# A two-layer hybrid-attention trunk on one NeuronCore: the first loads come as single blocks in the order of their use, and the rotary step works on both query tiles at once

## The chip, the cores and the metric

The kernel runs on one core of a Trainium2 chip. The metric is device time in microseconds (us), the median of several executions. The core has a matrix engine (TensorE, PE in the rows), whose weight loads are listed apart (PEld), a vector engine (VectorE, DVE), an activation engine (ScalarE, ACT), a general engine (GpSimd, POOL) and a sync engine (SP) that here only issues transfers (DMA) from DRAM to on-chip memory. Every engine works through its own instructions strictly in the order of the program; engines wait for each other and for transfers by semaphores.

## The reference, cut to what matters

One sequence of 256 tokens with 1024 channels goes through two layers. `h @ w_in` is one large projection whose column groups feed three attention branches; the rotary step (`apply_partial_rope`) turns the first 16 of 64 channels of some heads.

```
def apply_partial_rope(x, cos, sin):
    half = ROPE_DIM // 2
    xr = x[..., :ROPE_DIM].astype(jnp.float32)
    x1, x2 = xr[..., :half], xr[..., half:]
    rot = jnp.concatenate([x1 * cos - x2 * sin, x2 * cos + x1 * sin], axis=-1)
    return jnp.concatenate([rot.astype(x.dtype), x[..., ROPE_DIM:]], axis=-1)
...
    h = rms_norm(x, norm_g)
    proj = h @ w_in
...
    return x + merged @ w_out
```

## The kernel before, in words

The 256 tokens are two query tiles of 128 (`NT` = 2, index `t`); the 1024 channels are eight blocks of 128 (`KD` = 8, index `k`). Every matrix product keeps nearly full float32 precision: both operands are split into a rounded high part and the rest, and three products are added up (`mm3`, lines 297 to 299: high by high, high by low, low by high). The activations' parts are `hT` and `lT`; the weights' parts are `wh` and `wl`. A weight tile is 1024 columns wide and holds two blocks of 512 columns, or two of 384 to 396 columns, or four of 256; it is loaded into `st` (`load`, line 251), ScalarE rounds it into `wh` (line 275), and VectorE subtracts to get `wl` (line 276). `split` does that, four tiles ahead of TensorE (`AHEAD`). For the first tile alone the split is done block by block (line 272).

The program begins with `begin()` of layer 0, then `warm()`, which clears a scratch page `z` on VectorE (line 389) and multiplies it by itself on TensorE (line 392), then `x_cols(k)`, which makes `hT` on ScalarE (line 403) and `lT` on VectorE (line 404) from a transposed copy of the input `xt`, scaled by the gains of the norm. The product of the first projection is called `a` (`ps_a`): 8 blocks by 2 tiles by 3 products of 512 columns, 48 matrix products in all. Then come `mv`, `b`, `mq` and others of 384 to 396 columns, and between them `w0` to `w3` (`mm_w1`, lines 757 and 758), which multiply by `Z`.

When `ps_a` is complete, `post_a` takes it out of the accumulators, which needs the norm's factor `rt` (lines 326 to 331). It then scales heads into `qn` (line 497 for many heads, line 508 for one key head that is written twice), turns them by `rope` on GpSimd (lines 447 to 452), and TensorE transposes them against the identity matrix (line 460). The key heads are called `ns` (from `a`) and `nw` (from `b`, in `post_b`). ScalarE then makes `kh` (line 489) and VectorE `kl` (line 490).

The order of TensorE's instructions is the order of the code, which places background work by a clock of its own. The instructions of the other engines are put in order by a scheduler when the program is built: it may move one instruction ahead of another that stands earlier in the code. So the order on an engine is not read from the code.

Of the kernel before, what the change touches and what calls it, by code (L numbers as in the profile page):

```python
# [9 lines left out]
F32 = mybir.dt.float32  # L10
F32R = mybir.dt.float32r
AF = mybir.ActivationFunctionType
ALU = mybir.AluOpType
# [4 lines left out]
KD = D // 128  # L18
# [58 lines left out]
def lay_out(inputs):  # L77

    big = ("x", "w_in", "b_gate", "cmp_w1", "w_up_moba", "w_up_nsa", "w_up_fox", "w_out")
    a = {n: np.ascontiguousarray(inputs[n]) for n in big}  # L80
    a["first"] = np.concatenate([np.eye(128, dtype=np.float32), inputs["norm_g"].reshape(L * KD, 128).T], 1)
# [12 lines left out]
@with_exitstack  # L94
def trunk(ctx, tc, x, w_in, b_gate, cmp_w1, w_up_moba, w_up_nsa, w_up_fox, w_out, first_d, x_t, small_d, row_d, out):
    nc = tc.nc
    V, A, G, T = nc.vector, nc.scalar, nc.gpsimd, nc.tensor

# [16 lines left out]
    po = ctx.enter_context(tc.tile_pool(name="po", bufs=1, space=PSUM))  # L115


    first = const.tile([128, 144], F32, name="first")
    nc.scalar.dma_start(first, first_d)
    ident, ngc = first[:, 0:128], first[:, 128:144]  # L120
    xs = [const.tile([128, D], F32, name=f"x{t}") for t in range(NT)]

    def load_x(t):
# [22 lines left out]
        return bass.AP(tensor=src.tensor, offset=src.offset + off, ap=[list(d) for d in dims])  # L146

    def small_loads():
        nc.sync.dma_start(tabs[:, K_COS:K_W2], small_d[:, K_COS:K_W2])
        nc.sync.dma_start(row, bcast(row_d, 0, (0, 128), (1, R_END)))  # L150

# [96 lines left out]
                out_ += [(w_, i) for i in range(w_["m"])]  # L248
        return out_

    def load(w_, eng):
        n = w_["n"]
        w_["st"] = wst.tile([128, 1024], F32, name="st")
        v = w_["st"][:, 0:w_["m"] * n].rearrange("p (k n) -> p k n", n=n)
        for r, a, b, src in w_["loads"]:
            eng.dma_start(v[r, a:b], src)

    def prefetch_loads(n):

        for w_ in tiles[:n]:  # L260
            load(w_, nc.scalar)

    def split(w_):
        if "st" not in w_:
            load(w_, nc.sync)
        n = w_["n"]
        c = w_["m"] * n
        sv = w_["st"][:, 0:c]
        wh = wsp.tile([128, 1024], F32R, name="wh")
        wl = wsp.tile([128, 1024], F32R, name="wl")  # L270
        w_["h"], w_["l"] = wh[:, 0:c], wl[:, 0:c]
        m = n if w_["at"] == 0 else c
        for i in range(0, c, m):
            h = w_["h"][:, i:i + m]
            A.activation(h, sv[:, i:i + m], AF.Copy)  # L275
            V.tensor_tensor(w_["l"][:, i:i + m], sv[:, i:i + m], h.bitcast(F32), op=ALU.subtract)  # L276

# [84 lines left out]
    def layer(l):  # L362
# [5 lines left out]
        def begin():  # L368
            if l == 0:
                x_loads()  # L370
                prefetch_loads(2)
            sh["pre"] = A.preload_act_table_set("natural_log_exp_and_others")
            after(sh["pre"], state["sigs"])
            sh["om"] = [pgs.tile([128, D], F32, name=f"om{i}", tag="page") for i in range(NT)]
            sh["ssq"] = sm.tile([128, NT], F32, name="ssq")
            sh["hT"] = new_T()
            sh["z"] = [pgs.tile([128, D], F32, name=f"z{t}", tag="page") for t in range(NT)]
# [8 lines left out]
        def warm():  # L386

            z = sh["z"][0][:, 0:256]
            V.memset(z, 0.0)
            ps = pat.tile([128, 512], F32, name="at")  # L390
            for _ in range(4):
                T.matmul(ps[:, 0:256], z[:, 0:128], z, start=True, stop=True)

        def x_loads():

            sh["xt"] = [pgs.tile([128, 4, S], F32, name="xt", tag="page") for _ in range(2)]
            for a, b in ((0, 2), (2, 4), (4, 8)):
                nc.sync.dma_start(sh["xt"][a // 4][:, a % 4:a % 4 + b - a, :], x_t[:, a:b, :])

        def x_cols(k):  # L400
            xt, h, lo = [a[:, k % 4, :] for a in (sh["xt"][k // 4], *sh["hT"][k // 4])]
            g = ngc[:, l * KD + k:l * KD + k + 1]
            A.activation(h, xt, AF.Copy, scale=g)
            V.scalar_tensor_tensor(lo, xt, g, h.bitcast(F32), op0=ALU.mult, op1=ALU.subtract)  # L404

        def start_r():
# [32 lines left out]
            V.tensor_tensor(rr, rr, sh["r"][:, :, None].to_broadcast([128, NT, nh]), op=ALU.mult)  # L439
            return rr  # L440

        def rope(q, key, t, nh):

            tab = sh["rtab"][key]
            a = wk.tile([128, 6, 16], F32, name="rp_a")[:, 0:nh]
            b = wk.tile([128, 6, 16], F32, name="rp_b")[:, 0:nh]
            G.tensor_tensor(a, q[:, :, 0:16], tab[:, t, 0, :][:, None, :].to_broadcast([128, nh, 16]), op=ALU.mult)
            G.tensor_tensor(b[:, :, 0:8], q[:, :, 8:16],
                            tab[:, t, 1, 0:8][:, None, :].to_broadcast([128, nh, 8]), op=ALU.mult)
            G.tensor_tensor(b[:, :, 8:16], q[:, :, 0:8],  # L450
                            tab[:, t, 1, 8:16][:, None, :].to_broadcast([128, nh, 8]), op=ALU.mult)
            G.tensor_tensor(q[:, :, 0:16], a, b, op=ALU.add)  # L452

        def cols_of(q, pairs, key):

# [34 lines left out]
            V.scalar_tensor_tensor(e, p3[:, 0, :], g, d.bitcast(F32), op0=ALU.mult, op1=ALU.subtract)  # L490

        def heads_scaled(ps, rr, col, nh, key):
            res = []
            for t in range(NT):
                q = wk.tile([128, 6, HD], F32, name="qn", bufs=4)[:, 0:nh]
                res.append(q)
                V.tensor_tensor(q, ps[t][:, col:col + nh * HD].rearrange("p (h d) -> p h d", d=HD),
                                rr[:, t, 0:nh][:, :, None].to_broadcast([128, nh, HD]), op=ALU.mult)
                if key in sh["rtab"]:
                    rope(q, key, t, nh)  # L500
            return res

        def shared_scaled(ps, col, rr, i, key):
            res = []
            for t in range(NT):
                q = wk.tile([128, 6, HD], F32, name="qn", bufs=4)[:, 0:2]
                res.append(q)
                V.tensor_scalar(q, ps[t][:, col:col + HD][:, None, :].to_broadcast([128, 2, HD]),
                                rr[:, t, i:i + 1], None, op0=ALU.mult)
                rope(q, key, t, 2)  # L510
            return res

        def new_ss():
            return sm.tile([128, NT, 8], F32, name="ss")
# [247 lines left out]
        def cmp_post():  # L762
# [20 lines left out]
            kc = sm.tile([16, 2, HD], F32, name="kc")[0:NCMP]  # L783
            vc = sm.tile([16, HD], F32, name="vc")[0:NCMP]
            ssc = sm.tile([16, 1], F32, name="ssc")[0:NCMP]
            rsc = sm.tile([16, 1], F32, name="rsc")[0:NCMP]
            jk = sm.tile([16, HD], F32, name="jk")[0:NCMP]
# [218 lines left out]
        def queue_loads():  # L1006
            for o in ORDER:
                name, b = o[:-1], int(o[-1])
                if name == "w":
                    parts[o] = load_w1(b)  # L1010
                else:
                    c0, n = PROJ[name]
                    m = 1 if l == 0 and o == "a0" else 2 if l == 0 and o == "a1" else 4
                    parts[o] = chunk([[(i, i + m, rows_of(w, 4 * b + i, 4 * b + i + m, c0, n))
                                       for i in range(0, 4, m)]], n)
            sh["gls"] = [load_gl(c) for c in range(6)]
            sh["ups"] = [load_up(n) for n in range(2)]
            sh["outs"] = load_out()
# [10 lines left out]
        def mm_first(starts):  # L1029
            ps = sh["ps_a"] = new_acc()  # L1030
            if l == 0:
                for k in range(KD):
                    dense(ps, sh["hT"], parts[f"a{k // 4}"][k % 4:k % 4 + 1], 512, ks=[k], ends=(k == 0, k == KD - 1))
                    if k + 4 < KD:
                        x_cols(k + 4)
                return
            for t in range(NT):
                finish(starts[t])
# [120 lines left out]
```

## Time and profile before

| what | us |
|---|---|
| median of three runs | 523.15 (523.08 to 523.24) |
| the profiled execution, its own time | 524.93 |
| its span, which all rows are counted in | 522.8 |
| TensorE busy, matrix products | 508.3 (97% of the span) |
| VectorE busy | 395.0 (76%) |
| ScalarE busy | 326.3 (62%) |
| GpSimd busy | 106.4 (20%) |

The busy share of TensorE comes from modelled ends of overlapping products, so it says that the engine is nearly always in use, not that it runs at its peak. The profiled execution took 2.1 us more than its span and 1.8 us more than the median.

### The profile page before, as it was taken

The numbers are of one execution on the slowest core, as the hardware profiler recorded it, in microseconds if no ns is written. First come the engines' busy times: TensorE is split into PE (matmuls) and PEld (weight loads), VectorE is DVE, ScalarE is ACT, GpSimd is POOL, SyncE is SP. The second block draws the span as 40 slices with busy tenths as digits, with TensorE's granted clock in tenths as the row PEclk, the third lists the DMA queues.
The fourth block names the chain that finished last, engine by engine and source line by source line (L and its number), as shares of the span: only waits on it lengthen the run. The fifth ranks groups of instructions, "written<-read, shape, count | busy, mean of one in ns | idle before, by whom it ended". The sixth has DMA issues, their size and how long they took to land.

```text
span 522.8 us, 8342 instructions
## 1 busy us (share of the span) xinstructions
PE 508.3 (97%) x2862; PEld 453.4 (87%) x2862; DVE 395.0 (76%) x804; ACT 326.3 (62%) x619; POOL 106.4 (20%) x166
## 2 busy tenths in 40 slices
PE   7999999999999999899999989999999999989997
PEld 4899899999888888788889979999988888878886
DVE  3898787789974558898487987768898754697953
ACT  4886686976584375644276966678756555655440
POOL 3754314000300004025102333030011000132300
PEclk8999999999999999999999989999999999999999
DMA  8998876445554433655447987546437542445502
GB/s 296 334 245 245 234 234 188 141 154 162 173 180 126 147 121 93 205 171 181 136 144 216 226 230 218 178 135 197 158 120 213 170 123 83 160 131 192 180 21 80
DMA packets 56602, 90.73 MB, mean 174 GB/s; under 512 B 3696, under 2 KB 30960, under 8 KB 56560
## 3 DMA queue, kind: packets, MB, share of 16 engines
q1 hardware_dynamic: 55840, 89.08, 56.4%
q10 hardware_dynamic: 720, 1.12, 0.6%
q8 instruction: 22, 0.36, 0.3%
q14 instruction: 20, 0.16, 0.1%
HBM read 89.14 MB, written 1.05 MB: 173 GB/s over the span
## 4 chain that ended last, share of the span: by engine, by line
PE 67%; issue 15%; DVE 7%; POOL 5%; ACT 4%; DMA 1%; ACTq 0%; DVEq 0%; POOLq 0%
PE acc L297 19%; PE acc L299 18%; PE acc L298 18%; DVE wl L276 3%; ACT wh L275 2%; PE at L568 2%; DMA st<-in_w_in_dram 1%; POOL qn L452 1%; DVE om L921 1%; PE at L550 1%; PE at L551 1%; PE at L348 1%; PE at L460 1%; PE o L758 1%; PE o L757 1%
## 5 line engine op out<-in xcount | busy, mean ns | idle before, releaser
L276 DVE TENSOR_TENSOR wl<-st,wh 128x1024 fp32r<-128x1024 f32 (+4 forms) x177 | 201.8, 1147 | 65.3 <-ACT wh L275 63.6
L275 ACT ACTIVATE wh<-st 128x1024 fp32r<-128x1024 f32 (+4 forms) x177 | 169.9, 966 | 98.4 <-PE acc L299 72.0
L297 PE MATMUL acc<-wh,hT 128*128 128x512 f32 (+3 forms) x576 | 223.8, 388 | 2.4 <-ACT wh L275 2.2
L299 PE MATMUL acc<-wh,lT 128*128 128x512 f32 (+3 forms) x576 | 210.4, 365 | 0.0
L298 PE MATMUL acc<-wl,hT 128*128 128x512 f32 (+3 forms) x576 | 209.7, 364 | 0.4 <-DVE wl L276 0.4
L299 PEld LDWEIGHTS acc<-wh,lT 128*128 128x128 f32 x576 | 108.6, 189 | 12.4 <-DVE lT L404 0.9
L297 PEld LDWEIGHTS acc<-wh,hT 128*128 128x128 f32 x576 | 109.4, 190 | 11.0 <-ACT wh L275 2.8
L298 PEld LDWEIGHTS acc<-wl,hT 128*128 128x128 f32 x576 | 109.4, 190 | 8.5 <-DVE wl L276 1.4
L563 ACT ACTIVATE p<-p,nm 128x128 f32<-128x128 f32 x80 | 35.5, 445 | 29.6 <-DVE nm L561 29.5
L920 POOL TENSOR_TENSOR z<-z,tmp 128x512 f32<-128x512 f32 x8 | 13.0, 1653 | 113.2 <-ACT tmp L917 113.2
L561 DVE CUSTOM_DVE_ANT_0 p<-at,tabs 128x128 f32<-128x128 f32 x80 | 24.1, 352 | 9.9 <-PE at L555 9.8
L956 POOL TENSOR_TENSOR mg<-mg,tmp 128x512 f32<-128x512 f32 x8 | 15.8, 1998 | 55.0 <-DVE tmp L955 55.0
L297 PE MATMUL acc<-wh,qkT 128*128 128x512 f32 x64 | 25.2, 394 | 0.0
L299 PE MATMUL acc<-wh,qkT 128*128 128x512 f32 x64 | 24.9, 390 | 0.0
L298 PE MATMUL acc<-wl,qkT 128*128 128x512 f32 x64 | 24.9, 389 | 0.0
L568 PE MATMUL at<-first,p 128*128 128x128 f32 x120 | 19.8, 274 | 0.3 <-ACT qkT L483 0.2
L660 POOL TENSOR_TENSOR om<-om,tmp 128x256 f32<-128x256 f32 x8 | 7.7, 985 | 58.1 <-DVE rs_a L330 50.3
L906 DVE SCALAR_TENSOR_TENSOR gl<-acc,rt,tmp 128x512 f32<-128x512 f32 x24 | 17.0, 743 | 1.1 <-PE o L580 1.1
L568 PEld LDWEIGHTS at<-first,p 128*128 128x128 f32 x120 | 15.0, 146 | 2.5 <-ACT qkT L483 0.6
L758 PE MATMUL o<-wl,Z 128*63 128x256 f32 x64 | 16.3, 289 | 0.9 <-DVE wl L276 0.9
L757 PE MATMUL o<-wh,Z 128*63 128x256 f32 x64 | 16.6, 295 | 0.0
L572 DVE COPY pt<-at 128x384 f32<-128x384 f32 x20 | 11.0, 551 | 7.0 <-PE at L568 6.8
(232 smaller groups left out, 710.0 us busy)
## 6 DMA issues: line engine op xcount, KB each, us to landing
st<-in_w_in_dram SPq DMA_DIRECT2D x54, 512.0 KB, 3.4
st<-in_w_in_dram SPq DMA_DIRECT2D x56, 384.0 KB, 3.9
st<-in_cmp_w_dram SPq DMA_DIRECT2D x32, 256.0 KB, 4.2
st<-in_w_out_dram SPq DMA_DIRECT2D x16, 512.0 KB, 3.8
st<-in_w_in_dram SPq DMA_DIRECT2D x8, 396.0 KB, 6.9
st<-in_w_in_dram SPq DMA_DIRECT2D x8, 390.0 KB, 3.3
tmp<-in_b_gate_dram SPq DMA_DIRECT2D x12, 256.0 KB, 4.4
st<-in_w_up_moba_dram SPq DMA_DIRECT2D x4, 512.0 KB, 3.7
```

Source lines behind the costliest of these rows:

```text
L275: A.activation(h, sv[:, i:i + m], AF.Copy)
L276: V.tensor_tensor(w_["l"][:, i:i + m], sv[:, i:i + m], h.bitcast(F32), op=ALU.subtract)
L297: T.matmul(ps, sh, wh, start=first, stop=False)
L298: T.matmul(ps, sh, wl, start=False, stop=False)
L299: T.matmul(ps, sl, wh, start=False, stop=last)
L561: V.tensor_tensor_reduce(out=u, in0=sp, in1=tabs[:, K_MASK + 256 - nk:K_MASK + 256], scale=-SCALE, scalar=BIG, op0=ALU.add, op1=ALU.min, a ...
L563: exps.append(A.activation(u, u, AF.Exp, bias=nm, scale=-1.0, accum_out=rsum[:, t, hb:hb + 1]))
L568: T.transpose(pts[:, s * 128:(s + 1) * 128], p[:, s * 128:(s + 1) * 128], ident)
L757: T.matmul(U, st, h, start=i == 0, stop=False)
L758: T.matmul(U, st, lo, start=False, stop=i == CL - 1)
L906: V.scalar_tensor_tensor(sh["gl"][t][b][:, n * 512:(n + 1) * 512], ps[t], sh["r"][:, t:t + 1], bg, op0=ALU.mult, op1=ALU.add)
L956: (G if b == 1 else V).tensor_tensor(m, m, tmp, op=ALU.add)
```

## The change

Three edits. The identity matrix and the norm's gains, one transfer before, become two, and the identity comes later. The first loads are issued as single blocks in the order in which the first projection uses them, from two queues, and the first four weight tiles (eight blocks) are split block by block; block 0 of `hT` is made on VectorE, and `warm()` has five products in place of four. The rotary step handles both query tiles in one set of four operations in place of two sets. Some small buffers get one copy in place of two.

```
-    first = const.tile([128, 144], F32, name="first")
-    nc.scalar.dma_start(first, first_d)
-    ident, ngc = first[:, 0:128], first[:, 128:144]
+    ngc = const.tile([128, L * KD], F32, name="ngc")
+    nc.scalar.dma_start(ngc, gains_d)
+    ident = const.tile([128, 128], F32, name="ident")
...
     def small_loads():
+        nc.sync.dma_start(ident, eye_d)
...
-    def load(w_, eng):
+    def load(w_, queues):
...
-        for r, a, b, src in w_["loads"]:
-            eng.dma_start(v[r, a:b], src)
-
-    def prefetch_loads(n):
-
-        for w_ in tiles[:n]:
-            load(w_, nc.scalar)
+        for i, (r, a, b, src) in enumerate(w_["loads"]):
+            queues[i % len(queues)].dma_start(v[r, a:b], src)
...
-        m = n if w_["at"] == 0 else c
+        m = n if w_["at"] < 4 else c
...
-                prefetch_loads(2)
...
-            for _ in range(4):
+            for _ in range(5):
                 T.matmul(ps[:, 0:256], z[:, 0:128], z, start=True, stop=True)
...
-            for a, b in ((0, 2), (2, 4), (4, 8)):
+
+            def xk(a, b):
                 nc.sync.dma_start(sh["xt"][a // 4][:, a % 4:a % 4 + b - a, :], x_t[:, a:b, :])
+            xk(0, 1)
+            load(tiles[0], (nc.scalar, nc.sync))
+            xk(1, 2)
+            xk(2, 3)
+            load(tiles[1], (nc.scalar, nc.sync))
+            xk(3, 4)
+            load(tiles[2], (nc.sync,))
+            xk(4, 8)
+            load(tiles[3], (nc.sync,))
...
-            A.activation(h, xt, AF.Copy, scale=g)
+            if k == 0:
+                V.tensor_scalar(h, xt, g, None, op0=ALU.mult)
+            else:
+                A.activation(h, xt, AF.Copy, scale=g)
...
-        def rope(q, key, t, nh):
+        def rope(q, key, nh):
...
-            G.tensor_tensor(a, q[:, :, 0:16], tab[:, t, 0, :][:, None, :].to_broadcast([128, nh, 16]), op=ALU.mult)
...
+            G.tensor_tensor(a, q[:, :, :, 0:16], tb(0, 0, 16), op=ALU.mult)
+            G.tensor_tensor(b[:, :, :, 0:8], q[:, :, :, 8:16], tb(1, 0, 8), op=ALU.mult)
+            G.tensor_tensor(b[:, :, :, 8:16], q[:, :, :, 0:8], tb(1, 8, 16), op=ALU.mult)
+            G.tensor_tensor(q[:, :, :, 0:16], a, b, op=ALU.add)
...
         def shared_scaled(ps, col, rr, i, key):
...
+            q = wk.tile([128, NT, 2, HD], F32, name="kn", bufs=1)
+            for t in range(NT):
+                V.tensor_scalar(q[:, t], ps[t][:, col:col + HD][:, None, :].to_broadcast([128, 2, HD]),
                                 rr[:, t, i:i + 1], None, op0=ALU.mult)
-                rope(q, key, t, 2)
-            return res
+            rope(q, key, 2)
+            return [q[:, t] for t in range(NT)]
...
-                    m = 1 if l == 0 and o == "a0" else 2 if l == 0 and o == "a1" else 4
+                    m = 1 if l == 0 and name == "a" else 4
...
-                    if k + 4 < KD:
-                        x_cols(k + 4)
...
-    for k in range(4):
+    for k in range(KD):
         layers[0]["x_cols"](k)
-        prefetch(k + 1)
+        prefetch(k // 2 + 1)
```

The order of instructions on the engines moves at three places that matter below. First, VectorE at the very start, before the change:

```order
L162 MEMSET ones_96 128x1
L389 MEMSET z_122 128x256
L404 SCALAR_TENSOR_TENSOR lT<-xt,first,hT 128x256
L276 TENSOR_TENSOR wl<-st,wh 128x512 x2
L404 SCALAR_TENSOR_TENSOR lT<-xt,first,hT 128x256
L276 TENSOR_TENSOR wl<-st,wh 128x1024
```

And VectorE at the same place with the change:

```order
L164 MEMSET ones_97 128x1
L273 TENSOR_TENSOR wl<-st,wh 128x512 x2
L385 MEMSET z_131 128x256
L410 TENSOR_SCALAR hT<-xt,ngc 128x256
L273 TENSOR_TENSOR wl<-st,wh 128x512
L413 SCALAR_TENSOR_TENSOR lT<-xt,ngc,hT 128x256 x3
L273 TENSOR_TENSOR wl<-st,wh 128x512
```

The clearing of the scratch page `z` stood second and now stands behind the low parts of weight blocks 0 and 1. TensorE's order begins with the products of `z`, five now, and then the first projection, as before.

Second, GpSimd in layer 1, where the key heads `nw` are turned, before the change:

```order
L447 TENSOR_TENSOR rp_a<-qn,rtab_nw 128x32
L448 TENSOR_TENSOR rp_b<-qn,rtab_nw 128x2x8
L450 TENSOR_TENSOR rp_b<-qn,rtab_nw 128x2x8
L452 TENSOR_TENSOR qn<-rp_a,rp_b 128x2x16
L447 TENSOR_TENSOR rp_a<-qn,rtab_nw 128x32
L448 TENSOR_TENSOR rp_b<-qn,rtab_nw 128x2x8
L450 TENSOR_TENSOR rp_b<-qn,rtab_nw 128x2x8
L452 TENSOR_TENSOR qn<-rp_a,rp_b 128x2x16
```

And with the change, with the next operation of GpSimd behind it:

```order
L459 TENSOR_TENSOR rp_a<-kn,rtab_nw 128x2x32
L460 TENSOR_TENSOR rp_b<-kn,rtab_nw 128x2x2x8
L461 TENSOR_TENSOR rp_b<-kn,rtab_nw 128x2x2x8
L462 TENSOR_TENSOR kn<-rp_a,rp_b 128x4x16
L459 TENSOR_TENSOR rp_a<-qn,rtab_mq 128x192
```

Four operations of double size stand in the place of eight; the first tile is ready only when both are.

Third, ScalarE in layer 0, behind the product `w1`, where it makes `kh` from the transposed heads `nw`, before the change (`sq` is the square of the projection `mq`):

```order
L275 ACTIVATE wh<-st 128x1024
L489 ACTIVATE kh_292<-at,tabs 128x128
L432 ACTIVATE sq<-acc,rt 128x384
L275 ACTIVATE wh<-st 128x1024
L275 ACTIVATE wh<-st 128x768
```

And with the change:

```order
L272 ACTIVATE wh<-st 128x1024
L499 ACTIVATE kh_305<-at,tabs 128x128
L272 ACTIVATE wh<-st 128x1024
L499 ACTIVATE kh_305<-at,tabs 128x128
L272 ACTIVATE wh<-st 128x768
```

The square `sq` no longer stands ahead of the next weight tile's high part.

## Rows read from the trace of the kernel before

**Rows 1.** The page, busy time of each engine (share of the span, instructions).

```profile
PE 508.3 (97%) x2862; PEld 453.4 (87%) x2862; DVE 395.0 (76%) x804; ACT 326.3 (62%) x619; POOL 106.4 (20%) x166
```

**Rows 2.** Whom TensorE waited for: total us, times, longest us.

```profile
PE at L460 <- POOL qn L452: 2.7, 4, 1.3
PE acc L297 <- ACT wh L275: 2.2, 1, 2.2
PE o L758 <- DVE wl L276: 0.9, 1, 0.9
```

**Rows 3.** Timeline of the start: start us, us, engine, line, out<-in; [idle before, releaser].

```profile
0.89 0.27 DVE L389 MEMSET z<- 128x256 f32 x1
...
1.22 3.64 PE L392 MATMUL at<-z 128*128 128x256 f32 x8 [1.22 <-DVE z L389]
...
6.40 0.63 ACT L275 ACTIVATE wh<-st 128x512 fp32r<-128x512 f32 x1 [0.67 <-DMA st<-in_w_in_dram]
...
7.08 0.50 PE L297 MATMUL acc<-wh,hT 128*128 128x512 f32 x1 [2.22 <-ACT wh L275]
...
18.50 0.39 PE L297 MATMUL acc<-wh,hT 128*128 128x512 f32 x1
...
21.22 0.33 PE L297 MATMUL acc<-wh,hT 128*128 128x384 f32 x1
```

**Rows 4.** Windows of the start: busy us of each engine, PEclk, DMA share, GB/s.

```profile
3.00:4.00 1.00, 1.00 (x4) 0.73 (x3) 0.00 (x0) 0.72 (x1) 0.96 (x2) 1.00 0.82 219
7.00:8.00 1.00, 0.70 (x2) 0.38 (x3) 0.69 (x1) 0.03 (x1) 0.00 (x0) 1.00 1.06 408
...
10.00:11.00 1.00, 1.00 (x4) 0.81 (x3) 0.12 (x1) 0.75 (x1) 0.00 (x0) 0.50 1.06 394
...
12.00:13.00 1.00, 0.79 (x3) 0.19 (x1) 1.00 (x3) 1.00 (x3) 0.17 (x1) 1.00 1.00 353
```

**Rows 5.** Transfers of the first 22 us: count, KB each, median us to landing.

```profile
xt<-in_x_t_dram SPq DMA_DIRECT2D x2, 256.0 KB, 4.6
...
first<-in_first_dram ACTq DMA_DIRECT2D x1, 72.0 KB, 4.5
```

**Rows 6.** Groups of the first 22 us by shape: busy us, mean ns | idle before.

```profile
L404 DVE SCALAR_TENSOR_TENSOR lT<-xt,first,hT 128x256 fp32r<-128x256 f32 x8 | 3.6, 476 | 4.6 <-ACT hT L403 4.6
...
L276 DVE TENSOR_TENSOR wl<-st,wh 128x512 fp32r<-128x512 f32 x2 | 1.4, 692 | 2.1 <-ACT wh L275 2.1
...
L275 ACT ACTIVATE wh<-st 128x512 fp32r<-128x512 f32 x2 | 1.3, 630 | 2.0 <-DMA st<-in_w_in_dram 2.0
```

**Rows 7.** Timeline of layer 0 behind the first projection.

```profile
22.54 0.37 ACT L428 ACTIVATE kv<-acc,rt 128x128 f32<-128x128 f32 x1 [0.27 <-DVE rt L331]
...
36.18 0.44 PE L460 MATMUL at<-first,qn 128*128 128x128 f32 x2 [0.34 <-POOL qn L452]
...
55.31 0.33 PE L758 MATMUL o<-wl,Z 128*63 128x256 f32 x1 [0.93 <-DVE wl L276]
```

**Rows 8.** Timeline of layer 1 where the heads `nw` are turned.

```profile
302.72 0.61 DVE L508 TENSOR_SCALAR qn<-acc,rr 128x128 f32<-128x128 f32 x2
303.15 0.25 POOL L447 TENSOR_TENSOR rp_a<-qn,rtab_nw 128x32 f32<-128x32 f32 x1 [10.83 <-DVE qn L508]
303.25 4.22 DVE L276 TENSOR_TENSOR wl<-st,wh 128x768 fp32r<-128x768 f32 x4
303.36 0.94 POOL L448 TENSOR_TENSOR rp_b<-qn,rtab_nw 128x16 f32<-128x16 f32 x1
...
304.27 1.19 POOL L450 TENSOR_TENSOR rp_b<-qn,rtab_nw 128x16 f32<-128x16 f32 x1
...
305.54 1.11 POOL L452 TENSOR_TENSOR qn<-rp_a,rp_b 128x32 f32<-128x32 f32 x1
...
306.70 0.33 PE L460 MATMUL at<-first,qn 128*128 128x128 f32 x1 [1.28 <-POOL qn L452]
...
308.32 0.46 PE L460 MATMUL at<-first,qn 128*128 128x128 f32 x1 [0.77 <-POOL qn L452]
```

**Rows 9.** Window of layer 1 right behind that place; columns as in rows 4.

```profile
309.00:312.00 3.00, 3.00 (x16) 2.90 (x15) 1.69 (x3) 2.22 (x4) 0.00 (x0) 0.54 1.09 225
```

More of the change, by code (lines that the diff above doesn't have):

```diff
@@ L80, in lay_out @@
     a = {n: np.ascontiguousarray(inputs[n]) for n in big}
-    a["first"] = np.concatenate([np.eye(128, dtype=np.float32), inputs["norm_g"].reshape(L * KD, 128).T], 1)
+    a["gains"] = inputs["norm_g"].reshape(L * KD, 128).T
+    a["eye"] = np.eye(128, dtype=np.float32)
     a["x_t"] = inputs["x"][0].T.reshape(KD, 128, S).transpose(1, 0, 2)
@@ L94, in trunk @@
 @with_exitstack
-def trunk(ctx, tc, x, w_in, b_gate, cmp_w1, w_up_moba, w_up_nsa, w_up_fox, w_out, first_d, x_t, small_d, row_d, out):
+def trunk(ctx, tc, x, w_in, b_gate, cmp_w1, w_up_moba, w_up_nsa, w_up_fox, w_out, gains_d, eye_d, x_t, small_d, row_d, out):
     nc = tc.nc
@@ L254, in load @@
         v = w_["st"][:, 0:w_["m"] * n].rearrange("p (k n) -> p k n", n=n)
-        for r, a, b, src in w_["loads"]:
-            eng.dma_start(v[r, a:b], src)
-    def prefetch_loads(n):
-        for w_ in tiles[:n]:
-            load(w_, nc.scalar)
+        for i, (r, a, b, src) in enumerate(w_["loads"]):
+            queues[i % len(queues)].dma_start(v[r, a:b], src)
     def split(w_):
         if "st" not in w_:
-            load(w_, nc.sync)
+            load(w_, (nc.sync,))
         n = w_["n"]
@@ L440, in head_factors, with tb @@
             return rr
-        def rope(q, key, t, nh):
+        def rope(q, key, nh):
             tab = sh["rtab"][key]
-            a = wk.tile([128, 6, 16], F32, name="rp_a")[:, 0:nh]
-            b = wk.tile([128, 6, 16], F32, name="rp_b")[:, 0:nh]
-            G.tensor_tensor(a, q[:, :, 0:16], tab[:, t, 0, :][:, None, :].to_broadcast([128, nh, 16]), op=ALU.mult)
[L448 to L452, printed above, removed]
+            def tb(i, c0, c1):
+                return tab[:, :, i, c0:c1][:, :, None, :].to_broadcast([128, NT, nh, c1 - c0])
+            a = wk.tile([128, NT, 6, 16], F32, name="rp_a", bufs=1)[:, :, 0:nh]
+            b = wk.tile([128, NT, 6, 16], F32, name="rp_b", bufs=1)[:, :, 0:nh]
+            G.tensor_tensor(a, q[:, :, :, 0:16], tb(0, 0, 16), op=ALU.mult)
+            G.tensor_tensor(b[:, :, :, 0:8], q[:, :, :, 8:16], tb(1, 0, 8), op=ALU.mult)
+            G.tensor_tensor(b[:, :, :, 8:16], q[:, :, :, 0:8], tb(1, 8, 16), op=ALU.mult)
+            G.tensor_tensor(q[:, :, :, 0:16], a, b, op=ALU.add)
         def cols_of(q, pairs, key):
@@ L492, in heads_scaled @@
         def heads_scaled(ps, rr, col, nh, key):
-            res = []
+            q = wk.tile([128, NT, 6, HD], F32, name="qn")[:, :, 0:nh]
             for t in range(NT):
-                q = wk.tile([128, 6, HD], F32, name="qn", bufs=4)[:, 0:nh]
-                res.append(q)
-                V.tensor_tensor(q, ps[t][:, col:col + nh * HD].rearrange("p (h d) -> p h d", d=HD),
+                V.tensor_tensor(q[:, t], ps[t][:, col:col + nh * HD].rearrange("p (h d) -> p h d", d=HD),
                                 rr[:, t, 0:nh][:, :, None].to_broadcast([128, nh, HD]), op=ALU.mult)
-                if key in sh["rtab"]:
-                    rope(q, key, t, nh)
-            return res
+            if key in sh["rtab"]:
+                rope(q, key, nh)
+            return [q[:, t] for t in range(NT)]
         def shared_scaled(ps, col, rr, i, key):
-            res = []
+            q = wk.tile([128, NT, 2, HD], F32, name="kn", bufs=1)
             for t in range(NT):
-                q = wk.tile([128, 6, HD], F32, name="qn", bufs=4)[:, 0:2]
-                res.append(q)
-                V.tensor_scalar(q, ps[t][:, col:col + HD][:, None, :].to_broadcast([128, 2, HD]),
+                V.tensor_scalar(q[:, t], ps[t][:, col:col + HD][:, None, :].to_broadcast([128, 2, HD]),
                                 rr[:, t, i:i + 1], None, op0=ALU.mult)
-                rope(q, key, t, 2)
-            return res
+            rope(q, key, 2)
+            return [q[:, t] for t in range(NT)]
         def new_ss():
@@ L782, in cmp_post @@
                              w2s[:, l, kv, c, :], start=c == 0, stop=c == 1)
-            kc = sm.tile([16, 2, HD], F32, name="kc")[0:NCMP]
-            vc = sm.tile([16, HD], F32, name="vc")[0:NCMP]
+            kc = sm.tile([16, 2, HD], F32, name="kc", bufs=1)[0:NCMP]
+            vc = sm.tile([16, HD], F32, name="vc", bufs=1)[0:NCMP]
             ssc = sm.tile([16, 1], F32, name="ssc")[0:NCMP]
             rsc = sm.tile([16, 1], F32, name="rsc")[0:NCMP]
-            jk = sm.tile([16, HD], F32, name="jk")[0:NCMP]
+            jk = sm.tile([16, HD], F32, name="jk", bufs=1)[0:NCMP]
             A.activation(vc, ps[0:NCMP, HD:2 * HD], AF.Copy)
```

## The prediction

> **What bounds the kernel now.** I read the busy shares first: TensorE is in use 97% of the span [rows 1]. In such a kernel only time in which TensorE stands still, or runs at its lower clock, can be won or lost. So I read next whom TensorE waited for [rows 2], then the timeline of the two places that the change touches, the start [rows 3 to 6] and the rotary step [rows 7, 8].
>
> At the start the reader should see three things. The scratch products begin at 1.22, right behind the clearing of `z` at 0.89, and are over long before the first weight block has landed: they cost nothing. The first real product starts at 7.08, released by the high part of weight block 0, which ScalarE began at 6.40 after waiting for the transfer. And the first projection ends at 21.22, where the 384-column products begin [rows 3]. At full clock its 48 products need 48 x 0.227 = 10.9 us (12 of them from 18.50 to 21.22 take 2.72), so 14.1 - 10.9 = 3.2 us of its 14.1 us are lower clock and waits; the granted clock was 0.50 at 10 to 11 us and 1.00 again at 12 to 13 [rows 4], that is 1.2 and 2.4 GHz.
>
> The rotary step makes TensorE wait 2.7 us in all [rows 2]: 1.28 + 0.77 for the two `nw` tiles of layer 1 [rows 8], 0.34 at 36.18 in layer 0 [rows 7], and the remaining 0.3 for `nw` in layer 0.
>
> **The start, step by step.** The order of VectorE decides it. `z` is now cleared behind the low parts of blocks 0 and 1, so the scratch products, which stand first on TensorE, wait for two weight blocks to land and be split, and all the real work waits behind them.
>
> When do blocks 0 and 1 land? Before, block 0 had landed by 6.4 [rows 3], with 72 KB, two input pieces of 256 KB and itself on the way, 840 KB. Now 8 KB of gains, 128 KB of input and two weight blocks of 256 KB must come, 648 KB. The 192 KB less are 0.5 us at 408 GB/s [rows 4]: 5.9. Bounds: 5.0, where the first input piece landed before (issue at 0.74 plus about 4.3; the median of two is 4.6 [rows 5]), and 6.4, if the number of pieces counts and not their bytes. I take 5.9, since the rate was steady once transfers flowed.
>
> Then two high parts at 0.63, one low part at 0.69 [rows 6], the clearing at 0.27 [rows 3] and some 0.1 of hand-overs: 5.9 + 1.26 + 0.69 + 0.27 + 0.1 = 8.2 us for the first scratch product, in place of 1.2. Four of them took 3.64 us [rows 3], 0.91 each, so five take 4.55, to 12.8. I let the clock rise as long after the engine's start as before (from 7.08 to between 11 and 12, say 4.2 us): it rises at 12.4, the last 0.4 runs at double speed, and the real products begin at 12.6. They find all parts ready. From 8.2 VectorE has one high part (some 0.4 us), six low weight parts and eight low input parts to make, 0.4 + 6 x 0.69 + 8 x 0.48 = 8.4 us [rows 6], about 1.05 us for each of the eight blocks, where TensorE takes 1.36 for each. Without that cover each late part would cost up to the 2.2 us of block 0 in [rows 2]; I count none. So the projection ends at 12.6 + 10.9 = 23.5 in place of 21.2: **+2.3 us**. With landing at 5.0 and the clock 0.7 us earlier it is +1.0; with landing at 6.4 and a clock that rises some 3 us later (seven products at 0.2 us more each) it is +4.0.
>
> This delay is passed on in full, since what TensorE waits for later hangs on its own earlier products. It wins a little back. Before, the first projection was done 1.3 us before `rt` let its accumulators be emptied (21.22 against 22.54 [rows 7]); now `rt` has 2.3 us more, so heads come earlier against TensorE's stream and the wait of 0.34 at 36.18 goes: **-0.3** (bounds 0 and -0.34).
>
> **The wait at 55.31** (0.93 for a low weight part [rows 7]) is fed by ScalarE, where the square of `mq` stood ahead of that weight tile's high part. It is moved behind it, but the `kh` on which both wait stays. I take **-0.4**, about half; bounds 0 and -0.93.
>
> **The rotary step in layer 1.** Eight GpSimd operations become four. An undisturbed one of 32 elements takes 0.25 us [rows 8], so one set would take some 1.2 us. But the next three took 0.94, 1.19 and 1.11: VectorE ran four low weight parts from 303.25 (4.22 us, 1.055 each), and GpSimd finished one operation behind each [rows 8]. VectorE's order there is unchanged. The merged set can start only behind the second `qn`, which ends at 303.33, no longer ahead of the first low part. Its four operations then end behind the four low parts, the last at about 303.25 + 4.22 + 0.2 = 307.7, in place of 306.7 for the first tile. TensorE, which before stood until 306.70 and then until 308.32, with three products between, stands once, until 307.7, does the same three products (0.5 us), and goes on at 308.2: **0**, bounds +0.9 and, if GpSimd slips through, -2.05 and the clock with it. The granted clock was 0.54 at 309 to 312 behind these two waits [rows 9]; that lost 3 x 0.46 = 1.4 us. A single stall of 2.2 us is as long as the two, so I keep that loss. `nw` in layer 0 has the same trade: 0, bounds -0.3 and +0.4. For the other heads GpSimd was done before TensorE asked; a merged set has the same work ahead of the same product.
>
> The new small buffers, and the identity that lands later, are needed first by the transposes behind `mv0`: nothing, hidden by the first projection's 48 products.
>
> **The sum:** +2.3 - 0.3 - 0.4 + 0 = +1.6 us on the profiled execution, whose own time is 524.93 for a span of 522.8; as a difference it goes on the median: 523.15 + 1.6 = **524.8 us**. A difference under about 0.2% (1.05 us) can't be told from no change.
>
> **Rivals.**
>
> *The merged rotary step pays (faster).* If GpSimd's four operations in layer 1 run undisturbed, they end near 303.4 + 1.4 = 304.8, before TensorE asks at 305.42 (306.70 - 1.28 [rows 8]). Then 2.05 us of waiting and the 1.4 us of clock are won: 524.8 - 3.5 = 521.3 us. For it speaks the 0.25 us of an undisturbed operation, against it the three stretched ones. It decides at whether VectorE's low weight parts run between 303.4 and 305.4.
>
> *The start costs little (no change).* Blocks 0 and 1 land at 5.0 and the clock rises early: +1.0 in place of +2.3, so 523.5 us, no change that can be measured. For it speaks that far fewer bytes stand ahead; against it the slow first microseconds, 219 GB/s at 3 to 4 us [rows 4], which smaller pieces don't shorten by themselves.
>
> *Small pieces load slower (slower still).* If the first 648 KB come at 219 GB/s in place of 408, that is 3.0 in place of 1.6 us, and everything behind moves: 524.8 + 1.4 = 526.2 us. Against it speaks that pieces of 256 KB already moved at 408 GB/s with others in flight [rows 4].
>
> The Trainium skill (DMA: Bandwidth & Descriptors, Bandwidth) speaks for this rival: it wants at least 1 MiB in a transfer and lists 138 GB/s at 64 KB and 341 at 1 MB. By an estimate of 200 GB/s from that page the first blocks would land some 1.6 us later and the time be 526.4 us; the trace does not agree, with 408 GB/s at 7 to 8 us [rows 4].
>
> **How the numbers follow.** The forecast has 0.60, the paying rotary step 0.15, the cheap start 0.15, slow loading 0.10. Slower by over 0.2%: 0.60 + 0.10 = 0.70; within: 0.15; faster: 0.15. The range takes in the cheap start, with a little of the rotary step's gain, and the slow loading: 522.2 to 526.7; it leaves out most of the rotary rival and the far end of the slow start, under 0.2 together.
>
> **What would show it.** Right: scratch products that begin near 8 us, behind two low weight parts; a first projection without waits at full clock that ends near 23.5; no wait for the rotary step at its first place in layer 0; one stall near 2 us for `nw` in layer 1, with GpSimd's operations stretched to about 1 us. Wrong: scratch products that are over before the first block has landed, a first projection that ends before 21 us, or a merged rotary set of under 2 us in layer 1.

## The result and the profile after

The changed kernel took 527.34 us (median of four runs, 526.31 to 527.46), the kernel before 523.19 (four runs); ratio 1.0069 [1.0052, 1.0085]. It is slower, by 4.1 us at the medians; 1.6 were forecast. Timed again later (run f1 below) it took 526.88 us (median of ten runs) beside 523.61 for 27 runs of the kernel before, ratio 1.0046 [1.0029, 1.0064]. Why the distance differs between these two is half of what follows. The profiled execution after took 526.31 us for a span of 524.5, the fastest of its four; the one before had taken 524.93, more than any of the four. So the two traces lie only 1.4 us apart (1.7 in span).

The page of the changed kernel, busy time of each engine, to be held against [rows 1]:

```profile
PE 505.7 (96%) x2864; PEld 453.3 (86%) x2864; DVE 396.9 (76%) x808; ACT 326.4 (62%) x621; POOL 96.7 (18%) x126
```

GpSimd has 40 instructions and 9.7 us less, the merged rotary step; it is not what bounds the kernel. Whom TensorE waited for in the changed kernel (as [rows 2]):

```profile
PE at L388 <- DVE z L385: 7.6, 1, 7.6
...
PE at L470 <- POOL kn L462: 2.6, 2, 2.4
PE at L470 <- POOL qn L462: 0.6, 1, 0.6
PE at L470 <- ACT nqT L695: 0.6, 1, 0.6
PE o L764 <- DVE wl L273: 0.5, 1, 0.5
```

The 7.6 us ahead of the scratch products are no loss by themselves, since no block had landed for most of them. The rest tells the story: `nw` in layer 1 (now in a tile `kn`) is one stall of 2.4 in place of 1.28 and 0.77, and two waits of 0.6 are new. The timeline of the start (as [rows 3]):

```profile
5.30 1.67 ACT L272 ACTIVATE wh<-st 128x512 fp32r<-128x512 f32 x3 [1.88 <-DMA st<-in_w_in_dram]
5.96 1.29 DVE L273 TENSOR_TENSOR wl<-st,wh 128x512 fp32r<-128x512 f32 x2 [5.10 <-ACT wh L272]
...
7.26 0.27 DVE L385 MEMSET z<- 128x256 f32 x1
...
7.59 4.53 PE L388 MATMUL at<-z 128*128 128x256 f32 x10 [7.59 <-DVE z L385]
...
11.66 0.69 PE L294 MATMUL acc<-wh,hT 128*128 128x512 f32 x1
...
22.54 0.37 ACT L437 ACTIVATE kv<-acc,rt 128x128 f32<-128x128 f32 x1 [1.34 <-DVE rt L328]
...
22.87 0.33 PE L294 MATMUL acc<-wh,hT 128*128 128x384 f32 x1
```

As forecast, `z` is cleared behind two low parts, the scratch products come behind the first blocks, and the first projection then runs without a wait. The first block is there at 5.30 (forecast 5.9), and the projection ends at 22.87 (forecast 23.5, before 21.22 [rows 3]), 1.65 us later. `rt` lets the accumulators be emptied at 22.54, where it did before [rows 7]; that the two agree to the hundredth is chance, since f1, the same kernel, has 22.32. Layer 1, where the heads `nw` are turned (as [rows 8]):

```profile
304.39 0.61 DVE L514 TENSOR_SCALAR kn<-acc,rr 128x128 f32<-128x128 f32 x2
304.92 4.33 DVE L273 TENSOR_TENSOR wl<-st,wh 128x768 fp32r<-128x768 f32 x4
...
305.15 0.90 POOL L459 TENSOR_TENSOR rp_a<-kn,rtab_nw 128x64 f32<-128x64 f32 x1 [13.48 <-DVE kn L514]
306.02 1.23 POOL L460 TENSOR_TENSOR rp_b<-kn,rtab_nw 128x32 f32<-128x32 f32 x1
307.21 1.23 POOL L461 TENSOR_TENSOR rp_b<-kn,rtab_nw 128x32 f32<-128x32 f32 x1
308.51 0.91 POOL L462 TENSOR_TENSOR kn<-rp_a,rp_b 128x64 f32<-128x64 f32 x1
...
309.48 0.48 PE L470 MATMUL at<-ident,kn 128*128 128x128 f32 x1 [2.42 <-POOL kn L462]
...
310.72 0.41 PE L470 MATMUL at<-ident,kn 128*128 128x128 f32 x1
```

GpSimd's four operations take 305.15 to 309.42, one behind each of VectorE's four low parts, as forecast, and TensorE stands until 309.48. A stretch of low clock lies behind it, as before [rows 9]:

```profile
306.00:309.00 3.00, 1.06 (x6) 0.74 (x5) 3.00 (x3) 0.74 (x1) 2.92 (x4) 0.97 0.64 172
309.00:312.00 3.00, 2.52 (x9) 2.33 (x10) 1.03 (x3) 1.21 (x3) 0.43 (x1) 0.50 0.95 238
```

Put beside each other product by product, the two profiled executions differ by +4.6 us at the first real product, +1.8 at the 27th (17.89 against 16.10), +0.8 at the first place of the rotary step (36.94 against 36.18), +0.7 at 56 us, +1.5 at the heads of `mq` (67.81 against 66.32) and +1.5 at the end. The difference is made in the first 70 us, half of it by the start and half at the heads of `mq`; layer 1, where both executions have the low clock, adds nothing to it. Where the rest of the 4.1 us comes from, the runs below show.

### The profile page after: what moved, and what is told of

Its sections match the earlier page's. It is cut to its first block, busy times and chain, and to the rows that moved or that the text cites. A ratio compares the mean times of both kernels' runs of the same rounds, so it can differ in the third digit from the quotient of the medians.

```text
span 524.5 us, 8308 instructions
## 1 busy us (share of the span) xinstructions
PE 505.7 (96%) x2864; PEld 453.3 (86%) x2864; DVE 396.9 (76%) x808; ACT 326.4 (62%) x621; POOL 96.7 (18%) x126
## 4 chain that ended last, share of the span: by engine, by line
PE 79%; DVE 8%; ACT 5%; issue 4%; POOL 2%; DMA 1%; DVEq 0%; ACTq 0%; SPq 0%; POOLq 0%
PE acc L294 21%; PE acc L296 20%; PE acc L295 20%; DVE wl L273 4%; PE at L574 2%; ACT wh L272 2%; PE at L556 2%; PE at L557 2%; PE at L470 1%; DVE om L927 1%; PE o L582 1%; PE o L584 1%; PE o L586 1%; PE at L345 1%; ACT p L569 1%
## 5 line engine op out<-in xcount | busy, mean ns | idle before, releaser
L574 PE MATMUL at<-ident,p 128*128 128x128 f32 x120 | 19.8, 274 | 0.3 <-ACT qkT L493 0.2
L574 PEld LDWEIGHTS at<-ident,p 128*128 128x128 f32 x120 | 15.0, 146 | 2.4 <-ACT qkT L493 0.6
```

The lines of the kernel that those rows point to most:

```text
L574: T.transpose(pts[:, s * 128:(s + 1) * 128], p[:, s * 128:(s + 1) * 128], ident)
```

## The experiments

Fifteen runs: each part of the change alone (e1 to e4), the place in layer 1 taken out of the comparison (f1 to g1), and the start once more without it (g2 to h3). Runs with one letter shared a chip and the runs of the kernel before.

**e1, the changed kernel with `z` cleared first.**

```
         def begin():
             if l == 0:
+                sh["z"] = [pgs.tile([128, D], F32, name=f"z{t}", tag="page") for t in range(NT)]
+                V.memset(sh["z"][0][:, 0:256], 0.0)
                 x_loads()
...
         def warm():
-            V.memset(z, 0.0)
```

> The changed kernel, with the scratch page cleared as VectorE's first instruction, so that the five scratch products run at 1 to 6 us again; all else stays. Theory (the scratch products stand behind the weight split and hold up all real work): the first real product starts near 7.6 in place of 11.7, the first projection ends near 18 in place of 22.9, then TensorE waits longer at its first transposes, since rt still comes near 22.4; 522 to 524.5 us. Rival A (the merged rotary step costs the time) and rival B (the single-block loads cost it): 526.5 to 527.5 us, as the changed kernel.

Measured: 527.86 us (six runs, 525.90 to 529.48), 1.0067 [1.0045, 1.0089]. Nothing is won, although the real products begin at 7.54 us.

**e2, the changed kernel without scratch products** (`layers[0]["warm"]()` left out: products of zeros that no output uses).

> The changed kernel without any scratch products (they feed nothing). Theory: the first real product starts near 7.5, runs at the lower clock for some 4 us (about 2 us lost), and the first projection ends near 20.5; 523 to 525 us, clearly under the changed kernel. Rivals A and B: no gain, 526.5 us or more, since the clock's rise is only moved onto real products.

Measured: 527.96 us (six runs, 526.49 to 529.78), 1.0072 [1.0053, 1.009]. Nothing won either. So the theory that the placing of the scratch products is the loss fell with these two.

**e3, the new start with the old rotary step** (`rope`, `heads_scaled` and `shared_scaled` as before).

> The changed kernel with the rotary step of before (two sets of four operations). Theory: the merged step is worth nothing, 526.5 to 527.8 us. Rival A: 523 to 524.5 us.

Measured: 525.7 us, 1.0024 [1.0014, 1.0034]. **e4, the kernel before with the merged rotary step** (the same three functions of the changed kernel, and the smaller buffers).

> The kernel of before with the merged rotary step alone. Theory: one stall of about 2.2 us for nw in layer 1 in place of two of 2.05 together; 522.7 to 523.9 us. Rival A: 525.5 us or more. The rival of the prediction (the merged step pays): 519.7 to 521 us.

Measured: 524.28 us, 1.0005 [0.9993, 1.0017]: no change. So the new start costs something by itself (1.28 us by means), and the merged step costs nothing on the old start but something on the new one: some 2 us by the first result, 1.0 by the means of f1 below. The two do not add up. The first place to look was the stall in layer 1, where the times scatter.

**f1 to f4, and g1: `nw` in layer 1 asked for later.** TensorE's stall is taken away by one number of the code's own clock:

```
-            yield 8.0
+            yield 11.0 if l else 8.0
             for t in range(NT):
                 shared_cols(ks[t], 1, t, "nw")
```

f1 is the changed kernel as it is; f2 the changed kernel with this line, f3 that with the old rotary step, f4 the kernel before with this line alone, g1 that with the merged rotary step.

> The changed kernel as it is, timed once more beside the three below. If the 4.1 us at the medians are the change and not the mixture of runs with one, two or three low-clock stretches, it lies again 0.6 to 0.9% above the kernel before. If a good part was the mixture, it lies at 0.3 to 0.5%, 1.5 to 2.7 us above: the new start's 1.0 to 1.3 us (run e3) and the rotary step's share on top.

> The changed kernel with the two nw transposes of layer 1 asked for 3 us later in the planner's count (11.0 for 8.0). Theory A: the merged rotary step costs its time at this one stall (2.4 us until 309.48, and the low clock behind it, 1.4 us): the wait goes, and the time falls 2.5 to 4 us below the changed kernel as it is. Theory B: the cost lies ahead of it, in the waits at 43 and 68 us and in the start: the stall goes as well, but the time falls under 1.5 us, since the wait had covered work that then is waited for elsewhere.

> The new start with the old rotary step and the same later asking in layer 1. Under theory A (the merged step costs time at that stall alone) it ends level with the changed kernel with later asking, within 0.5 us. Under theory B it stays 1 us or more below it, by what the merged step costs at 43 and 68 us.

> The kernel before with the same later asking and nothing else. If the two stalls there (1.28 and 0.77 us) and the clock behind them (1.4 us) are lost time, it wins 2 to 3.5 us. It then also stands below all the others, by the 1.0 to 1.7 us of the new start. If the stalls only stood in for other waits, it is level with the kernel before.

> The kernel before with the merged rotary step and the later asking in layer 1, old start. If the merged step costs nothing but at the layer-1 stall, it is level with the kernel before with later asking alone (2.5 to 2.9 us under the kernel before). If it costs 0.6 us wherever it stands, as on the new start (wait for qn at 68 us), it is 1.8 to 2.3 us under the kernel before.

| run | median us | mean less the mean of before | ratio |
|---|---|---|---|
| f1 | 526.88 | +2.24 | 1.0046 [1.0029, 1.0064] |
| f2 | 522.62 | -1.41 | 0.9975 [0.9961, 0.9989] |
| f3 | 522.03 | -2.01 | 0.9967 [0.9958, 0.9977] |
| f4 | 520.94 | -3.12 | 0.9949 [0.9934, 0.9963] |
| g1 | 520.97 | -3.25 | 0.9935 [0.9920, 0.9950] |

The line wins 3.1 us (means) in the kernel before and 3.65 in the changed one; by the scatter of the runs the second figure is uncertain by 1.0 (95%, as all such figures below), so the two are not told apart. The windows of f4 at that place, the columns as in rows 4:

```profile
306.00:309.00 3.00, 3.00 (x25) 2.92 (x24) 3.00 (x5) 2.31 (x4) 2.92 (x5) 1.00 0.85 266
309.00:312.00 3.00, 3.00 (x20) 2.96 (x19) 2.95 (x9) 2.89 (x7) 0.00 (x0) 1.00 1.08 234
```

TensorE never stands and the clock stays at 1.00, 2.4 GHz, where [rows 9] had 0.54. The same windows of f1, the changed kernel itself in an execution of 525.1 us:

```profile
306.00:309.00 3.00, 1.10 (x6) 0.78 (x5) 3.00 (x3) 0.78 (x1) 2.92 (x4) 1.00 0.68 199
309.00:312.00 3.00, 2.50 (x19) 2.43 (x20) 1.43 (x5) 1.98 (x5) 0.44 (x1) 1.00 0.91 238
```

The stall is there (2.39 us), the low clock is not: 19 products lie in 309 to 312 where the profiled execution of 526.31 had nine. So behind the same stall the clock falls in some executions and not in others, and the times of one kernel come in groups. The mean granted clock of a run counts the stretches of low clock, not their places (leaving aside the last few us, where every trace has some): before's profiled execution, at 0.993, has two, at 8 to 11 and at 308 to 312 us; f4's, at 0.997, has only the first, the changed kernel's, at 0.996, only the second, and f1's, at 1.000, neither. On this chip the runs at 1.000 took 524.41 to 525.10 (changed, four runs) and 522.99 to 523.70 (before, twelve), medians 524.89 and 523.37, 1.5 apart. The runs with low clock took 526.78 to 527.85 (changed, 0.996 and 0.997, six) and 524.65 to 524.99 (before, 0.993, ten), medians 527.34 and 524.90, 2.4 apart. The other five runs of before, at 0.996 and 0.997, took 523.40 to 523.84 (four) and 526.69; no trace tells where their low clock lay. Without the stall no group is left in f4: 520.72 to 521.41, at clocks from 0.997 to 1.000. The changed kernel's distance between groups, 2.4 us, is more than the 1.2 us between its two profiled executions (526.31 and 525.1). A second place that differs from one execution to the next is the start, which f1 and f2 have in common: in f2's trace the first three real products run below full speed, in f1's only part of the first. The windows show a clock of 1.00 there in both, so this is read off the products, which follow each other at 0.42 us in f2, as they do before where the clock is 0.50 [rows 4], and at 0.23 later. From f2, with the end of the first projection:

```profile
12.00 0.99 PE L294 MATMUL acc<-wh,hT 128*128 128x512 f32 x1
12.79 0.63 PE L295 MATMUL acc<-wl,hT 128*128 128x512 f32 x1
13.21 0.58 PE L296 MATMUL acc<-wh,lT 128*128 128x512 f32 x1
13.63 0.40 PE L294 MATMUL acc<-wh,hT 128*128 128x512 f32 x1
...
23.85 0.33 PE L294 MATMUL acc<-wh,hT 128*128 128x384 f32 x1
```

and from f1, with the heads of `mq` as well:

```profile
11.54 0.58 PE L294 MATMUL acc<-wh,hT 128*128 128x512 f32 x1
11.96 0.39 PE L295 MATMUL acc<-wl,hT 128*128 128x512 f32 x1
12.19 0.39 PE L296 MATMUL acc<-wh,lT 128*128 128x512 f32 x1
12.43 0.40 PE L294 MATMUL acc<-wh,hT 128*128 128x512 f32 x1
...
22.64 0.33 PE L294 MATMUL acc<-wh,hT 128*128 128x384 f32 x1
...
67.85 0.55 PE L470 MATMUL at<-ident,qn 128*128 128x128 f32 x3 [0.57 <-POOL qn L462]
```

The fourth product begins 1.2 us later in f2, 0.46 of it because the scratch products did. At the heads of `mq` 0.9 us of this is left (68.75, shown below, against 67.85). That a slow start and the low clock in layer 1 come together in the runs near 527.3 would make the 2.4; no trace of such a run exists, so this is only argued.

The pair f3 and f2 shows what else the merged step costs: 0.6 us by means (uncertain by 0.5), and the wait that goes with it stands at the heads of `mq` in layer 0; f3's trace has no such wait. GpSimd's last operation of the set and TensorE's wait, from f2:

```profile
67.50 1.19 POOL L462 TENSOR_TENSOR qn<-rp_a,rp_b 128x192 f32<-128x192 f32 x1
...
68.75 0.55 PE L470 MATMUL at<-ident,qn 128*128 128x128 f32 x3 [0.58 <-POOL qn L462]
```

and from g1, on the old start:

```profile
64.74 0.60 POOL L453 TENSOR_TENSOR qn<-rp_a,rp_b 128x192 f32<-128x192 f32 x1
...
66.42 0.49 PE L461 MATMUL at<-first,qn 128*128 128x128 f32 x3
```

In g1 the last operation ran while VectorE had no low part (64.1 to 65.6) and took 0.60 us; in f2 VectorE's next low part began at 67.22 and the operation took 1.19. In g1 the set was over 1.08 us before TensorE's products, in f2 they waited 0.58 for it. That fits the merged step being free on the old start (g1 against f4: 520.97 and 520.94 us) and not on the new one.

**g2 to g4: `z` cleared first, now without the stall.** g2 is f2 and g3 is f3 with the edit of e1; g4 is g3 with the input's row loads issued ahead of the small tables.

```
-    small_loads()
     for t in range(NT):
         load_x(t)
+    small_loads()
```

> The changed kernel with z cleared first and the later asking. Without the layer-1 stall the pair with run f2 (z cleared late) tells what the late scratch products cost by themselves. Theory A: the late scratch products cost the 1.65 us by which the first projection ends later: 521.0 or less, 1.5 us under f2. Theory B: what follows hangs on other things (rt, the order of VectorE), so the gain is used up by 60 us: within 0.7 us of f2 or above it.

> As the run before, with the old rotary step. Beside run f3 it tells the same of the late scratch products without the merged step. If the early scratch products do harm only with the merged step, this one is 0.5 to 1.5 us under f3, at 520.5 to 521.5; if the order of ScalarE and VectorE in 30 to 60 us is at fault, it is level with f3 or above.

> As the run before, with the four row loads of the input issued ahead of the identity and the small tables, so that rt comes earlier and its operations stand two low weight parts earlier on VectorE. If the heads' chain behind rt uses up the early start, this wins 0.5 to 1.5 us more and may end under 520.9, the kernel before with later asking. If the chain is held elsewhere, no difference of over 0.4 us.

Measured: g2 523.86 us, 0.9993 [0.9983, 1.0004]; g3 523.55, 0.9987 [0.9976, 0.9997]; g4 523.6, 0.9991 [0.9980, 1.0002]. Early scratch products are 1.2 us (g2 against f2, by means against the shared kernel before) and 1.45 us (g3 against f3) worse than late ones, and earlier rows change nothing. Whom TensorE waited for in g3:

```profile
PE acc L294 <- DVE hT L412: 2.5, 1, 2.5
PE o L769 <- DVE wl L273: 2.0, 3, 0.9
...
PE acc L294 <- DVE qn L519: 0.7, 1, 0.7
```

g3 is 3.0 us ahead of f3 at the 27th real product (16.00 against 18.99), and behind it from 57 us on: it stands three times for a low part of the blocks `w0` to `w3`. ScalarE's timeline of g3 shows what holds the first of them:

```profile
30.51 1.05 ACT L439 ACTIVATE v<-acc,rt 128x384 f32<-128x384 f32 x2
33.49 1.36 ACT L743 ACTIVATE Z<-zf 64x256 fp32r<-64x256 f32 x2 [1.92 <-DVE zf L737]
34.88 1.81 ACT L272 ACTIVATE wh<-st 128x1024 fp32r<-128x1024 f32 x2
```

ScalarE stands 1.92 us for the second `zf`, with two high parts of those blocks behind it; in f4 the same two run at 31.99, and the second `Z` only at 35.65, behind them. Clearing `z` earlier thus also changed the order that the scheduler writes for ScalarE and VectorE, far behind the start.

**h1 to h3: late scratch products, or none, in the old order of loads.** All three have the later asking. In h1 `warm()` stands behind the first two blocks' `x_cols`, so that `z` is cleared behind the first low part of the input; h2 has no scratch products; h3 is f4 again.

```
     layers[0]["begin"]()
-    layers[0]["warm"]()
     for k in range(4):
         layers[0]["x_cols"](k)
         prefetch(k + 1)
+        if k == 1:
+            layers[0]["warm"]()
```

> The kernel before with later asking in layer 1, and z cleared behind the first low part of the input, so that the scratch products start when the first blocks have landed (6 to 7 us in place of 1.2) and the first real product near 10.5 in place of 7.25. Theory A, the late first product is what the new start costs: 1 to 1.5 us above the kernel before with later asking (some 522.0 to 522.5, 1.1 to 1.6 us below the kernel before). Theory B, the new start's cost is the other order of ScalarE and VectorE behind it: within 0.5 us of the kernel before with later asking.

> The kernel before with later asking, and no scratch products at all (left out: 4 products of zeros, which no output uses). If products ahead of the first block only pass the time, the same 520.9 within 0.4 us. If they bring the clock up earlier, 0.7 to 2 us more, with a lower granted clock in more of the first projection.

> The kernel before with later asking, once more on this chip, to stand beside the two above: again 2.5 to 3.3 us below the kernel before, and no run above 521.6, since the place at which the low clock could come has no stall any more.

Measured: h1 521.29 us, 0.9947 [0.9930, 0.9964]; h2 520.32, 0.9929 [0.9913, 0.9944]; h3 520.80, 0.9937 [0.9922, 0.9953]. In h1's trace the scratch products stand late, and the first projection ends nearly as early as before (rows of TensorE):

```profile
6.56 3.78 PE L392 MATMUL at<-z 128*128 128x256 f32 x8 [6.56 <-DVE z L389]
9.78 0.99 PE L297 MATMUL acc<-wh,hT 128*128 128x512 f32 x1
...
21.53 0.33 PE L297 MATMUL acc<-wh,hT 128*128 128x384 f32 x1
```

Its first real product is 2.6 us later than h3's (7.15), but from the fourth product on it runs at 0.23 us each, where h3's does from the ninth, and the end of the projection is only 0.33 later (21.20 in h3). By 36 us h1 is ahead: `rt` comes earlier in its order of VectorE (`kv` at 21.05 against 22.15), and its second transposes of heads stand at 35.57 against 36.15. The 0.5 us by which h1 is slower at the medians are lost behind that, at the heads `nw` of layer 0, where h3 stands 0.35 us and then 0.93 for a low part at 55.29:

```profile
52.23 0.33 PE L460 MATMUL at<-first,qn 128*128 128x128 f32 x1 [1.28 <-POOL qn L452]
...
53.84 0.33 PE L460 MATMUL at<-first,qn 128*128 128x128 f32 x1 [0.76 <-POOL qn L452]
```

So h1 shows that late scratch products by themselves cost next to nothing in the old order of loads, 0.33 us at the end of the projection and nothing by 36 us; what a projection costs that ends 1.65 us later it does not test. h2 is the fastest kernel of all, 3 us below the kernel before and 0.45 below h3 by means (uncertain by 0.3): in this order of loads products of zeros ahead of the first block win nothing once the stall is gone. Leaving them out also takes an instruction from VectorE's order, so the 0.45 need not be the products themselves.

## Why the forecast was right in its direction and too small

**The step that failed is the last one of the sum**, "as a difference it goes on the median: 523.15 + 1.6". The sum had kept the loss of clock behind the stall in layer 1 in both kernels ("so I keep that loss"), and the profiled execution of 524.93 has it. The three runs with the median 523.15, by their times, do not: 523.08 to 523.24 lie in the group of runs at full clock. The sum belonged on 524.93, which gives 526.5; the profiled execution after took 526.31. All four runs after have the low clock in their records (0.996 and 0.997), and of the four before, by their times, at most one; so the medians are 4.1 apart where the means of run f1's chip are 2.24 apart. The two means tell the rest: before's 27 runs have a mean of 524.07, 0.9 above 523.19, and the changed kernel's ten have 526.32, 1.0 below 527.34; 2.24 + 0.9 + 1.0 = 4.1. So 1.9 of the 4.1 us are chance, which executions each median happened to get. That the change makes the low clock more frequent (six of ten runs in f1, ten to fifteen of 27 before) is not shown.

**The terms by means.** New start: +1.1 (f3 against f4, uncertain by 0.4), forecast +1.6. Merged step outside layer 1's place: +0.6 (f2 against f3, uncertain by 0.5), forecast 0. Layer 1's place: 3.65 in the changed kernel and 3.11 in the one before (each with and without the later asking), +0.54, which is within the noise (uncertain by some 1.1); forecast 0. These add up to f1's 2.24 by construction; the forecast was 1.6. That the sum comes so near, and nearer still between the two traces (1.4 us), is in part luck: the start was put too high, and the wait of `mq` was put at nothing.

**The start.** Its rows were forecast well: landing 5.30 (5.9), scratch products from 7.59 (8.2), real products from 11.66 (12.6), end 22.87 (23.5), no waits in between, and 0.23 us for each product from 12.19 on. Executions of the same start differ by 1.2 us at its end, though (22.64 in f1, 23.85 in f2), and the upper bound, +4.0, adds up to 4.2 from its own parts. But "this delay is passed on in full" is wrong: of 1.65 us at the end of the projection 0.76 were left at 36.18 us. The wait of 0.34 there went as forecast; the other half microsecond went between 23 and 36 us, not at one wait that the rows show. What follows hangs on `rt` too, and `kv` begins at 22.54 in both: before, the projection was over 1.3 us ahead of that, so part of the delay fell into time that was waited for anyway. Where that reserve is used up, a delay is passed on for the most part: f2's `kv` waits for TensorE (23.37), and of the 1.2 us between f1 and f2 0.9 are left at `mq`. What of the start's 1.1 us is lateness, what a slow clock at the start of some executions (the first projection of f3's trace, its slowest run, ends at 23.97) and what the scheduler's other order, is not separated: no kernel here has the new loads with the old order of ScalarE and VectorE.

**The wait at 55.31**: 0.93 became 0.48, -0.45 for the forecast's -0.4. But the wait of 0.61 for `nqT`, at 43.28, is new and was not forecast, and the two about cancel: the traces are 0.7 us apart at 41.9 us and again at 56.

**The rotary step in layer 1.** The mechanism is as forecast: stretched operations, one stall, until 309.48; the forecast's 307.7 plus the 1.5 us that everything came later is 309.2. Not foreseen was that behind this stall the clock falls in some executions and not in others, and that `mq` would wait: "for the other heads GpSimd was done before TensorE asked" held for `mq` with the old start only.

**The stretched operations.** GpSimd's four operations take 0.90, 1.23, 1.23 and 0.91 us beside low parts of some 1.08 (4.33 for four), where one of 32 elements alone took 0.25 [rows 8], and their sum, 4.27, is that of the low parts, not of their elements. The Trainium skill (SBUF — State Buffer, SBUF: two separate sides) has VectorE operations with two inputs in SBUF, as the low parts are, and GpSimd operations that read SBUF take turns at one shared pair of ports, each holding it for its whole length; the rows agree.

**The rivals.** The paying rotary step was wrong: VectorE's low parts began at 304.92, ahead of GpSimd's first operation. The cheap start was half right: the first blocks landed at 5.30, most of the way to its 5.0, which left 1.65 of the 2.3 us, and part of that was won back behind the projection; by means the start costs 1.1. Slow loading was wrong: the first pieces were there at 5.30, with 298 GB/s at 3 to 4 us, where [rows 4] had 219:

```profile
3.00:4.00 1.00, 0.00 (x0) 0.00 (x0) 0.00 (x0) 0.42 (x1) 0.96 (x2) 1.00 0.94 298
```

The prediction's estimate of 200 GB/s, from the Trainium skill's figures by size (DMA: Bandwidth & Descriptors, Bandwidth), would have them some 1.6 us later than 5.9, and the trace does not agree. Those figures are for transfers issued from GpSimd; here pieces from two other queues were under way together.

## What to carry to other kernels

A sum that keeps a loss must be put on a time that contains it. Where the runs of one kernel fall into groups, first say in which group the profiled execution lies, and then compare like with like, or means over many runs. A delay at the start costs less where something that does not hang on it (here `rt`) comes later still; look for that reserve before passing the delay on. And where a stall shows behind operations that another engine stretches, ask later: one number in layer 1 won 3.1 us by means in the kernel before, more than the whole change cost (2.24).

## What the hardware did that was not expected

Behind a stall of 2.4 us in the same kernel the granted clock fell to 0.50 in 309 to 312 us of one execution and stayed at 1.00 in another. With that stall 22 of 27 runs of the kernel before lay in two groups, 522.99 to 523.70 and 524.65 to 524.99 us; without it all lay in one, 520.72 to 521.41. The recorded low clock at the start, by contrast, moves nothing that can be seen in f4: its runs at 0.997 took 520.94 and 520.95 us, the one at 1.000 took 520.76. In g2, g3 and g4 the runs with a recorded low clock were even the faster ones, by 0.5 to 0.8 us (g3: a mean of 523.48 for ten runs at 0.995 to 0.997, 524.27 for two at 1.000); in g3's trace it lies at the start. No run here explains that. So a mean clock tells groups apart only where a trace shows what its low stretches stand for.
